# Float32r transposes of DMA-copied tiles in a one-core decoder block

## The chip, the core and the metric

The kernel runs on one core of one Trainium2 chip. A core has TensorE (PE, which multiplies matrices and transposes; its weight loads are listed apart as PEld), VectorE (DVE), ScalarE (ACT), GpSimd (POOL) and SyncE (SP), each with its own queue of instructions worked off in order. SP, ACT and POOL can start DMA transfers from their queues. The metric is the device time of one launch in microseconds (us), the median of three runs.

## The reference

One decoder layer on 256 rows of width 2048, all float32. An RMS norm and one wide input projection feed two branches: sparse attention (each query keeps 64 of its causal keys by an indexer score) and retention, whose output is normed by heads and gated. Both branches are projected up, weighted by sigmoid gates, added, projected by `w_out` and added to the input. A second RMS norm and an MLP with a squared ReLU follow:

```python
proj = rms_norm(x, ln1_g) @ w_in
o_attn = dsa_attention(...)
o_ret  = silu(rg) * group_norm_heads(retention_chunkwise(rq, rk, rv), ret_gn_g, ret_gn_b)
merged = sigmoid(ga) * (o_attn @ w_up_attn) + sigmoid(gb) * (o_ret @ w_up_ret)
x = x + merged @ w_out
h2 = rms_norm(x, ln2_g)
return x + square(relu(h2 @ w_ff1)) @ w_ff2
```

The change moves numbers about; what is computed stays.

## The kernel before, in words

**Products in three parts.** Every large product is made from float32r operands in three passes. `split` (line 343) turns a weight tile into a rounded part `whi` (ACT, line 359) and a rest `wlo` (DVE, line 360); activations are split likewise. `products` (line 401) then issues three matmuls for each 128 x 128 block of the activation: hi x hi (line 405), hi x lo (406), lo x hi (407), each with 512 moving columns. Weights stream in from memory over SP's queue, `LOAD_AHEAD` = 8 items ahead, and are split two or three items ahead. An item is a pair of k slices of a weight tile.

**Why there are transposes.** An activation is made with its rows on the partitions, but the next product needs its columns there. So a made tile of 128 x 512 is transposed by TensorE in four blocks of 128 x 128 against an identity matrix (`ident`, a float32 slice of `csb`) into a PSUM tile `pt`, from which `split_into` (line 424) makes the hi and lo parts, ACT at line 429 and DVE at line 430. `transpose_in` (line 432, the transposes at line 438) serves the retention output (called at line 955), the merged tiles (line 1010) and the MLP's activations (`hidden`, line 1123). `next_norm` (line 1035) transposes the rows of the second norm itself, at line 1048, with evictions at line 1050.

**Where they stand in the order.** The program walks the products item by item. Jobs beside them are generators in a list `work`; `step()` moves each by one `yield`, and it runs once for every k slice in `run_block` (six products) and once for every item in the merged stages (six products for a first-layer item, twelve for a second-layer item). A `transpose_in` waits some yields before it transposes: two by default, `W_GN` = 7 after the retention; `next_norm` waits one. From this program order and the dependences the build lays out each engine's queue. It may move an instruction past others of its queue, so in the trace a transpose can stand within a triple of products.

**The MLP.** The hidden width is worked in eight groups (g = 0 to 7). The first group is a plain product (line 1129). For each later group the program alternates first-layer items, in a scheme of seven half products instead of eight (`first`, line 792), with second-layer items of the group before (`second`, line 1161); `merged` (line 123) writes this order out. A group gives four tiles of 128 x 512: two after the fifth half product, one after the sixth and one after the seventh. Each gets ReLU and Square on ACT (`squared`, lines 1110 and 1111), is transposed, and is read by the second-layer items of the next stretch. These items' results are scaled by ACT (line 1184) and added to memory by an accumulating DMA from POOL (line 1185).

**Buffers.** Tiles of 128 x 512 come from `stage()` (line 200), which hands out eight buffers in turn: three of four calls take one of six in the pool `sp`, the fourth takes one of two in the pool in `late["stg"]`. A buffer is written again only when the readers of its last tile are done.

Of the kernel before, what the change touches and what calls it, by code (L numbers as in the profile page):

```python
# [10 lines left out]
F32 = mybir.dt.float32  # L11
F32R = mybir.dt.float32r
I32 = mybir.dt.int32
AF = mybir.ActivationFunctionType
# [3 lines left out]
P = 128  # L18
# [4 lines left out]
BN = 512  # L23
# [10 lines left out]
FG = 8  # L34
NG = DFF // (FG * P)
# [124 lines left out]
def block_kernel(ctx, tc, cst, rot, xt, gains, w, x, ret_gn_g, ret_gn_b, out):  # L160
    nc = tc.nc
# [3 lines left out]
    cp = ctx.enter_context(tc.tile_pool(name="cp", bufs=1))  # L165
# [23 lines left out]


    W_NORM, W_SOFT, W_GN = 3, 5, 7
    n_stg, n_mid, n_sm = 8, {"ep": 12, "e4": 20}, 24
    late = {"ep": ep, "stg": ep}
    n_stage = [0]

    def nm(s):
        uid[0] += 1
        return f"{s}_{uid[0]}"

    def stage(shape=(P, BN)):  # L200
        n_stage[0] += 1
        pool, bufs = (late["stg"], 2) if n_stage[0] % 4 == 0 and "stg" in late else (sp, n_stg - 2)
        return pool.tile(list(shape), F32, tag="stg", name=nm("stg"), bufs=bufs)

    def mid(shape, dtype=F32):
        return late["ep"].tile(list(shape), dtype, tag="mid", name=nm("mid"), bufs=n_mid[late["ep"].name])

    def small(w):
        return sp.tile([P, w], F32, tag="small", name=nm("small"), bufs=n_sm)

    def psum_t():
        return PS["pt"].tile([P, BN], F32, tag="pt", name=nm("pt"))
# [4 lines left out]
    def act_pair(slot):  # L217
        a = ap[slot].tile([P, DK, 2, S], F32R, tag="act", name=nm("act"))
        return a[:, :, 0, :], a[:, :, 1, :], a

    work = []
# [17 lines left out]
    xsb = [stage() for _ in range(T * 4)]  # L239
    csb = cp.tile([P, C_DEC], F32, name="csb")  # L240
    ident = csb[:, C_ID:C_ID + P]
    cmk = csb[:, C_CM:C_CM + P]


# [144 lines left out]
    def run_block(key, act, before=None, ps=None, k0=0, k1=None):  # L389
        nk, n = B[key]  # L390
        ps = ps or [PS["pm"].tile([P, BN], F32, tag="pm", name=nm("pm")) for _ in range(T)]
        for k in range(k0, k1 or nk):
            if k % HC == 0:
                ws = weights((key, k // KC, k % KC // HC))
            if before:
                before(k)
            step()
            products(ps, [p[:, :n] for p in (ws[0][:, k % HC], ws[1][:, k % HC])], [act(k, t) for t in range(T)], k == 0, k == nk - 1)
        return [p[:, :n] for p in ps]
# [9 lines left out]
    def of(a):  # L409
        return lambda k, t: tuple(z[:, k, t * P:(t + 1) * P] for z in a[:2])  # L410


    def rsqrt(v, n, mul):

        a, y, u = small(n), small(n), small(n)
        nc.vector.tensor_scalar(a, v, mul, EPS, op0=ALU.mult, op1=ALU.add)
        nc.vector.tensor_scalar(y.bitcast(I32), a.bitcast(I32), -0.5, float(0x5F3759DF), op0=ALU.mult, op1=ALU.add)
        for _ in range(3):
            nc.vector.tensor_tensor(u, y, y, op=ALU.mult)
            nc.vector.scalar_tensor_tensor(u, u, -0.5, a, op0=ALU.mult, op1=ALU.mult)  # L420
            nc.vector.scalar_tensor_tensor(y, u, 1.5, y, op0=ALU.add, op1=ALU.mult)
        return y

    def split_into(act, k0, nk, t, ps):

        src = ps.rearrange("p (c i) -> p c i", c=nk)
        hi = act[0][:, k0:k0 + nk, t * P:(t + 1) * P]
        lo = act[1][:, k0:k0 + nk, t * P:(t + 1) * P]
        nc.scalar.activation(hi, src, AF.Copy)
        nc.vector.tensor_tensor(lo, src, hi.bitcast(F32), op=ALU.subtract)  # L430

    def transpose_in(act, k0, t, src, wait=2):

        for _ in range(wait):
            yield
        ps = psum_t()
        for c in range(4):
            nc.tensor.transpose(ps[:, c * P:(c + 1) * P], src[:, c * P:(c + 1) * P], ident)  # L438
        split_into(act, k0, 4, t, ps)


# [32 lines left out]
    def evict(dst, ps, t, func=AF.Copy):  # L474
        nc.scalar.activation(dst, ps, func, scale=rows[t])

    def evicted(ps, t):
        a = stage()
        evict(a, ps, t)
        return a  # L480
# [34 lines left out]
    for i in range(3):  # L515
        ps = run_block(("I", i), of(hT)) if i else psI
        for t in range(T):
            evict(iqs[:, t, i * IN:(i + 1) * IN], ps[t], t)
    mb = []

    def indexer():
        ik2 = mid([P, T, 2, ID])
# [70 lines left out]
    ps = run_block(("AV", 0), of(hT))  # L593
# [67 lines left out]
    for j in range(NKV):  # L661
        ps = run_block(("AQ", j), of(hT))
# [82 lines left out]
    def scaled(b):  # L745

        assert late["X2 made"]
        late["scaled"] = b + 1
        z = late["X2"][:, b // 2, b % 2 * 4:b % 2 * 4 + 4]
        hi, lo = (hT[a][:, 4 * b:4 * b + 4, P:] for a in range(2))  # L750
        nc.scalar.activation(hi, z, AF.Copy)
        nc.vector.tensor_tensor(lo, z, hi.bitcast(F32), op=ALU.subtract)

    for which, key in ((0, "RQ"), (1, "RK")):
        for i in range(2):
            last = (which, i) == (1, 0)
            ps = run_block((key, i), of(hT), before=(lambda k: scaled(k // 4 - 1) if k in (4, 8, 12) else None) if last else None)
# [93 lines left out]
    for gate, u in ((z, u) for z in BESIDE for u in range(2)):  # L851
# [10 lines left out]
        for item in beside(gate, u):  # L862
# [7 lines left out]
            else:  # L870
                branch(item, of(oT if gate == "GA" else hT))
                i = item[0][1] - 2 * u
# [13 lines left out]
    rT = act_pair(1)  # L886
# [45 lines left out]
    def normed(j, ys, gb, sg):  # L932
        mv, vr, nb = small(4 * T), small(2 * T), small(2 * T)
        for t in range(T):
            for a in range(2):
                st = small(6)
                nc.vector.bn_stats(st, ys[t][:, a * RV:(a + 1) * RV])
                nc.vector.bn_aggr(mv[:, 4 * t + 2 * a:4 * t + 2 * a + 2], st)
        mean, var = (mv.rearrange("p (a b) -> p a b", b=2)[:, :, i] for i in range(2))
        nc.vector.tensor_copy(vr, var)  # L940
        yield
        r = rsqrt(vr, 2 * T, 1.0)
        nc.vector.scalar_tensor_tensor(nb, mean, -1.0, r, op0=ALU.mult, op1=ALU.mult)
        yield
        for t in range(T):
            y = ys[t]
            for a in range(2):
                c = slice(a * RV, (a + 1) * RV)
                i = 2 * t + a
                nc.scalar.activation(y[:, c], y[:, c], AF.Identity, scale=r[:, i:i + 1], bias=nb[:, i:i + 1])  # L950
            nc.vector.tensor_tensor(y, y, gb[0], op=ALU.mult)
            nc.vector.tensor_tensor(y, y, gb[1], op=ALU.add)
            yield
            nc.vector.tensor_tensor(y, y, sg[t], op=ALU.mult)
            work.append(transpose_in(rT, 4 * j, t, y, W_GN))

    for j in range(4):
        if j < 2:

            i = j  # L960
# [5 lines left out]
        for src in (ret_gn_g, ret_gn_b):  # L966
            g = mid([P, BN])
            nc.gpsimd.dma_start(g, src[:, j * BN:(j + 1) * BN].to_broadcast([P, BN]))
            gb.append(g)
        for t in range(T):  # L970
            z = mid([P, BN])
# [6 lines left out]
        ps = run_block(("RV", j), of(hT))  # L978
# [9 lines left out]
    mT = act_pair(0)  # L988
# [14 lines left out]
    for i in range(4):  # L1003
        ms = mss[i] if i in pair else gates(i)
        ps = run_block(("UR", i), of(rT), ps=pair.get(i), k0=len(PARTS[0]) * KC if i in pair else 0)
        for t, m in enumerate(ms):
            g = sgb[:, t, i * BN:(i + 1) * BN]
            nc.vector.tensor_tensor(g, ps[t], g, op=ALU.mult)
            nc.vector.tensor_tensor(m, m, g, op=ALU.add)
            work.append(transpose_in(mT, 4 * i, t, m))  # L1010


    x2 = px.tile([P, T, D], F32, tag="big2", name="x2")
# [21 lines left out]
    def next_norm(i):  # L1035

        xs = []
        for t in range(T):
            a = stage()
            nc.scalar.activation(a, x2[:, t, i * BN:(i + 1) * BN], AF.Copy, scale=rs[:, t:t + 1])  # L1040
            xs.append(a)
        yield
        half, c0 = divmod(4 * i, HK)
        for k in range(0, 4, 2):
            ps = psum_t()
            for c in range(2):
                for t in range(T):
                    nc.tensor.transpose(ps[:, (2 * c + t) * P:(2 * c + t + 1) * P], xs[t][:, (k + c) * P:(k + c + 1) * P], ident)
            for c in range(2):
                nc.scalar.activation(xr[half][:, :, c0 + k + c, :], ps[:, c * S:(c + 1) * S].rearrange("p (t s) -> p t s", t=T),  # L1050
                                     AF.Copy, scale=g2[:, 4 * i + k + c:4 * i + k + c + 1])
            yield
        for t in range(T):
            both(((X11, X21), (X12, X22))[half][t], xr[half][:, t:t + 1, c0:c0 + 4, :], 1, slice(c0, c0 + 4))
# [21 lines left out]
    for i in range(4):  # L1076
        ps = run_block(("O", i), of(mT))
        for t in range(T):
            z = x2[:, t, i * BN:(i + 1) * BN]
# [13 lines left out]
    hid = act_pair(0)  # L1093
# [26 lines left out]
    def form(f, k):  # L1120
        return tuple(xf[:, a, f, k, :] for a in range(2))

    def hidden(g, t, i):
        work.append(transpose_in([z[:, g % 2 * FG:] for z in hid[:2]], 4 * i, t, ys.pop((t, i))))

    blocks = ((X11, X21), (X12, X22))
    ys = {}
    for i in (1, 0):
        ps = run_block(("F1", i), lambda k, t: form(blocks[k // HK][t], k % HK))
# [107 lines left out]
```

## Time and profile before

| what | value |
|---|---|
| time, median of 3 runs | 1611.77 us (1611.72 to 1613.01) |
| span of the profiled execution, first to last instruction | 1609.7 us |
| time outside the span, against the median | 2.1 us |
| TensorE busy | 1603.1 us |
| TensorE's weight loads busy | 1334.0 us |
| VectorE busy | 1316.7 us |
| ScalarE busy | 1001.8 us |
| GpSimd busy | 90.9 us |
| moved by DMA | 351.80 MB |

The profiled execution is given by its span alone; what lies around it is taken as the 2.1 us by which the median is longer. A row of the page that groups instructions gives line, engine, operation, output <- inputs, shape and count, then busy time, mean length of one, and the engine's idle time just before with what ended it. A row of the chain of waits gives start, length, engine, output tile and line of a piece of the chain that ended last: the length there is what the piece adds to the end. A row of the timeline gives start, length as recorded, engine, line, operation and count; recorded lengths of matmuls overlap, since they are pipelined.

### The profile page before, as it was taken

The page shows a single profiled execution, that of the slowest core. Times are in us where ns is not written, and L with a number is a line of the kernel's source. Part 1 is how long each engine was busy: PE and PEld are TensorE (multiplying, and loading weights), DVE is VectorE, ACT ScalarE, POOL GpSimd, SP SyncE. Part 2 cuts the span into 40 slices and gives each one's busy share as a digit, 9 for nine tenths or more (in the row PEclk, how much of TensorE's full clock was granted, in tenths as well). Part 3 has the DMA queues.
Part 4 walks back from the last instruction along what each step waited for, and adds up shares of the span by engine and source line. Part 5 has one row for each costly group of instructions (what it writes and reads, how often), then busy time and mean ns, then how long its engine had stood idle before and what let it go on. Part 6 is the DMA issues. An engine that isn't in the chain of part 4 may idle for free.

```text
span 1609.7 us, 19743 instructions
## 1 busy us (share of the span) xinstructions
PE 1603.1 (100%) x7438; PEld 1334.0 (83%) x7438; DVE 1316.7 (82%) x1474; ACT 1001.8 (62%) x1236; POOL 90.9 (6%) x135
## 2 busy tenths in 40 slices
PE   9999999999999999999999999999999999999999
PEld 8978888888888888888888888888888888888887
DVE  6678889898989898688665589898989898989884
ACT  7556566566666666555444666766767676767672
POOL 0000000000000001202000000000000000000000
PEclk9999999999999999999999999999999999999999
DMA  9645346656565655857557574767676777777763
GB/s 331 221 148 183 131 144 248 220 216 230 202 257 207 264 200 181 320 202 261 184 203 255 204 274 145 248 197 254 207 250 198 241 227 235 235 235 234 218 201 133
DMA packets 68416, 351.80 MB, mean 219 GB/s; under 512 B 7776, under 2 KB 14560, under 8 KB 32736
## 3 DMA queue, kind: packets, MB, share of 16 engines
q1 hardware_dynamic: 51040, 308.96, 52.8%
q0 software_dynamic: 14256, 35.14, 10.0%
q10 hardware_dynamic: 3024, 6.44, 1.1%
q8 instruction: 58, 0.95, 0.2%
q14 instruction: 38, 0.31, 0.1%
HBM read 323.24 MB, written 27.26 MB: 218 GB/s over the span
## 4 chain that ended last, share of the span: by engine, by line
PE 96%; DVE 3%; DMA 0%; ACT 0%; issue 0%; ACTq 0%; DVEq 0%
PE pm L405 11%; PE pm L407 11%; PE pm L406 11%; PE pf L405 11%; PE pf L407 11%; PE pf L406 11%; PE pq L406 9%; PE pq L407 9%; PE pq L405 9%; PE pt L438 1%; DVE wlo L360 1%; PE pa L405 1%; PE pa L406 0%; PE pa L407 0%; PE pt L649 0%; PE pa L907 0%
## 5 line engine op out<-in xcount | busy, mean ns | idle before, releaser
L360 DVE TENSOR_TENSOR wlo<-raw,whi 128x1024 fp32r<-128x1024 f32 (+2 forms) x544 | 645.7, 1200 | 211.1 <-ACT whi L359 203.1
L359 ACT ACTIVATE whi<-raw 128x1024 fp32r<-128x1024 f32 (+2 forms) x544 | 563.3, 1042 | 406.5 <-PE pm L407 200.5
L405 PE MATMUL pm<-whi,act 128*128 128x512 f32 (+1 forms) x800 | 310.0, 388 | 0.3 <-ACT act L449 0.3
L406 PE MATMUL pm<-wlo,act 128*128 128x512 f32 (+1 forms) x800 | 306.5, 383 | 0.5 <-DVE wlo L360 0.5
L407 PE MATMUL pm<-whi,act 128*128 128x512 f32 (+1 forms) x800 | 307.0, 384 | 0.0
L405 PE MATMUL pf<-whi,act 128*128 128x512 f32 (+1 forms) x768 | 298.5, 390 | 0.0
L406 PE MATMUL pf<-wlo,act 128*128 128x512 f32 (+1 forms) x768 | 298.2, 388 | 0.0
L407 PE MATMUL pf<-whi,act 128*128 128x512 f32 (+1 forms) x768 | 298.1, 388 | 0.0
L360 DVE TENSOR_TENSOR wlo<-rawc,whi 128x1024 fp32r<-128x1024 f32 x176 | 214.7, 1220 | 43.6 <-ACT whi L359 41.4
L359 ACT ACTIVATE whi<-rawc 128x1024 fp32r<-128x1024 f32 x176 | 186.3, 1059 | 80.8 <-PE pf L407 35.8
L349 DVE TENSOR_TENSOR raw<-raw,raw 128x2048 f32<-128x2048 f32 x88 | 201.0, 2285 | 1.1 <-DMA raw<-in_w_dram 0.5
L407 PEld LDWEIGHTS pm<-whi,act 128*128 128x128 f32 x800 | 150.2, 188 | 27.8 <-DVE act L450 0.2
L405 PEld LDWEIGHTS pm<-whi,act 128*128 128x128 f32 x800 | 150.3, 188 | 26.9 <-ACT act L449 0.6
L406 PEld LDWEIGHTS pm<-wlo,act 128*128 128x128 f32 x800 | 150.3, 188 | 26.9 <-DVE wlo L360 1.1
L405 PEld LDWEIGHTS pf<-whi,act 128*128 128x128 f32 x768 | 144.1, 188 | 30.0 <-ACT whi L359 0.8
L407 PEld LDWEIGHTS pf<-whi,act 128*128 128x128 f32 x768 | 144.2, 188 | 29.8
L406 PEld LDWEIGHTS pf<-wlo,act 128*128 128x128 f32 x768 | 144.3, 188 | 29.5
L405 PE MATMUL pq<-whi,xf 128*128 128x512 f32 x392 | 154.4, 394 | 0.0
L407 PE MATMUL pq<-whi,xf 128*128 128x512 f32 x392 | 152.7, 390 | 0.0
L406 PE MATMUL pq<-wlo,xf 128*128 128x512 f32 x392 | 152.6, 389 | 0.0
L1185 POOL DMA_DIRECT2D sums<-ev x56 | 48.3, 943 | 777.2 <-ACT ev L1184 775.6
L407 PEld LDWEIGHTS pq<-whi,xf 128*128 128x128 f32 x392 | 73.6, 188 | 15.5
(206 smaller groups left out, 1520.3 us busy)
## 6 DMA issues: line engine op xcount, KB each, us to landing
raw<-in_w_dram SPq DMA_DIRECT2D x188, 1024.0 KB, 5.4
rawc<-in_w_dram SPq DMA_DIRECT2D x88, 1024.0 KB, 5.7
sums<-ev POOLq DMA_DIRECT2D x56, 256.0 KB, 5.5
raw<-in_w_dram SPq DMA_DIRECT2D x8, 736.0 KB, 4.8
raw<-in_w_dram SPq DMA_DIRECT2D x7, 512.0 KB, 7.0
raw<-in_w_dram SPq DMA_DIRECT2D x8, 368.0 KB, 7.4
stg<-in_x_dram SPq DMA_DIRECT2D x8, 256.0 KB, 7.6
rqkd<-stg POOLq DMA_DIRECT2D x8, 256.0 KB, 2.8
```

What stands on the lines that cost most here:

```text
L349: nc.vector.tensor_tensor(one, one, two, op=ALU.add)
L359: nc.scalar.activation(a, src, AF.Copy)
L360: nc.vector.tensor_tensor(b, src, a.bitcast(F32), op=ALU.subtract)
L405: nc.tensor.matmul(d, h, hi, start=first, stop=False, skip_group_check=skip)
L406: nc.tensor.matmul(d, h, lo, start=False, stop=False, skip_group_check=skip)
L407: nc.tensor.matmul(d, l, hi, start=False, stop=last, skip_group_check=skip)
L438: nc.tensor.transpose(ps[:, c * P:(c + 1) * P], src[:, c * P:(c + 1) * P], ident)
L1185: nc.gpsimd.dma_start(sums[:, t, i * BN:(i + 1) * BN], z, accum_op=ALU.add)
```

## The change

A float32r identity `unit` is made once, by an ACT copy of `ident`. A new helper `moved(src)` takes a stage tile of type float32r and starts a DMA on ACT's queue that copies `src` into it bit by bit. `turn` transposes a block: if the source is float32r, with `unit` and into the PSUM tile read as float32r; otherwise as before. Four callers use it:

- the retention's normed tiles, all copied; the wait goes from 7 yields to 10
- the merged tiles of blocks 0 to 2; their wait goes from 2 to `W_MOVED` = 6; those of block 3 stay as they were
- `next_norm`, all tiles; the wait goes from 1 to 6
- the MLP's tiles of all groups but the last; the wait goes from 2 to 6

```diff
+    W_MOVED = 6
...
-    def stage(shape=(P, BN)):
+    def stage(shape=(P, BN), dtype=F32):
         n_stage[0] += 1
         pool, bufs = (late["stg"], 2) if n_stage[0] % 4 == 0 and "stg" in late else (sp, n_stg - 2)
-        return pool.tile(list(shape), F32, tag="stg", name=nm("stg"), bufs=bufs)
+        return pool.tile(list(shape), dtype, tag="stg", name=nm("moved" if dtype == F32R else "stg"), bufs=bufs)
+
+    def moved(src):
+
+        z = stage(dtype=F32R)
+        nc.scalar.dma_start(z.bitcast(F32), src)
+        return z
...
+    unit = cp.tile([P, P], F32R, name="unit")
...
+    def turn(ps, c, src, i):
+
+        d, z = ps[:, c * P:(c + 1) * P], src[:, i * P:(i + 1) * P]
+        if src.dtype == F32R:
+            nc.tensor.transpose(d.bitcast(F32R), z, unit)
+        else:
+            nc.tensor.transpose(d, z, ident)
+
     def transpose_in(act, k0, t, src, wait=2):
...
         for c in range(4):
-            nc.tensor.transpose(ps[:, c * P:(c + 1) * P], src[:, c * P:(c + 1) * P], ident)
+            turn(ps, c, src, c)
         split_into(act, k0, 4, t, ps)
...
+    nc.scalar.activation(unit, ident, AF.Copy)
...
-            work.append(transpose_in(rT, 4 * j, t, y, W_GN))
+            work.append(transpose_in(rT, 4 * j, t, moved(y), W_GN + 3))
...
-            work.append(transpose_in(mT, 4 * i, t, m))
+            work.append(transpose_in(mT, 4 * i, t, *((moved(m), W_MOVED) if i < 3 else (m,))))
...
             nc.scalar.activation(a, x2[:, t, i * BN:(i + 1) * BN], AF.Copy, scale=rs[:, t:t + 1])
-            xs.append(a)
-        yield
+            xs.append(moved(a))
+        for _ in range(W_MOVED):
+            yield
...
-                    nc.tensor.transpose(ps[:, (2 * c + t) * P:(2 * c + t + 1) * P], xs[t][:, (k + c) * P:(k + c + 1) * P], ident)
+                    turn(ps, 2 * c + t, xs[t], k + c)
...
-        work.append(transpose_in([z[:, g % 2 * FG:] for z in hid[:2]], 4 * i, t, ys.pop((t, i))))
+        y = ys.pop((t, i))
+        work.append(transpose_in([z[:, g % 2 * FG:] for z in hid[:2]], 4 * i, t, *((moved(y), W_MOVED) if g < NG - 1 else (y,))))
```

## The prediction, on record before the result

> **What bounds the kernel now.** I read the page first, then busy time by stretches, then the chain of work in order of time around the transposes. The page:
>
> ```profile
> span 1609.7 us, 19743 instructions
> PE 1603.1 (100%) x7438; PEld 1334.0 (83%) x7438; DVE 1316.7 (82%) x1474; ACT 1001.8 (62%) x1236; POOL 90.9 (6%) x135
> ...
> DMA  9645346656565655857557574767676777777763
> ...
> PE 96%; DVE 3%; DMA 0%; ACT 0%; issue 0%; ACTq 0%; DVEq 0%
> PE pm L405 11%; PE pm L407 11%; PE pm L406 11%; PE pf L405 11%; PE pf L407 11%; PE pf L406 11%; PE pq L406 9%; PE pq L407 9%; PE pq L405 9%; PE pt L438 1%; DVE wlo L360 1%; PE pa L405 1%; PE pa L406 0%; PE pa L407 0%; PE pt L649 0%; PE pa L907 0%
> ```
>
> TensorE carries 96% of the chain, and the transposes of line 438 stand in it with 1%. A busy share alone does not say that nothing waits, so two stretches (length; PE, PEld, DVE, ACT, POOL busy; clock; DMA share; GB/s):
>
> ```profile
> 250.00:650.00 400.00, 399.96 (x1777) 330.19 (x1777) 360.47 (x322) 248.70 (x263) 23.79 (x42) 1.00 0.62 225
> 975.00:1609.00 634.00, 631.00 (x2860) 521.89 (x2858) 543.58 (x452) 429.30 (x488) 48.28 (x56) 1.00 0.68 216
> ```
>
> The clock is at 1.00 in both, and TensorE loses 0.04 us of 400 and 3 of 634. So what is taken off TensorE's stream shows in the time, one for one, as long as nothing new keeps it waiting. DVE, at 543.6 of 634 in the MLP, would be next, 87 us behind: far more than this change can move.
>
> **The price of a transpose.** The chain gives what one instruction costs the stream, not its latency (start, length, engine, tile, line):
>
> ```profile
> 689.95 0.23 PE pm L407
> ...
> 691.31 0.23 PE pm L407
> 691.54 0.44 PE pt L438 x4
> 691.98 0.23 PE pm L405
> ...
> 790.39 0.87 PE pt L438 x8
> ```
>
> Seven products of 512 columns lie between 689.95 and 691.54, 0.227 us each. Eight transposes of 128 columns take 0.87, 0.109 each, as do those at 691.54. All are float32; the products are float32r. A transpose in float32r is not in this trace, nor any float32r product of 128 columns. The nearest is 256 columns wide:
>
> ```profile
> L405 PE MATMUL pa<-mid,mid 128*128 128x256 f32 x24 | 6.8, 281 | 0.0
> ```
> ```profile
> 671.63 0.12 PE pa L405
> ...
> 672.34 0.24 PE pm L405
> ```
>
> Six of these fill 671.63 to 672.34, 0.118 each. So 256 columns are worth 0.227 - 0.118 = 0.109, and 128 fewer would make 0.118 - 0.054 = 0.064. That is the middle value. The bounds come from the weight loads, since each transpose needs one:
>
> ```profile
> 114.30 0.19 PEld L406 LDWEIGHTS pm<-wlo,act 128*128 128x128 f32 x1 [0.88 <-DVE wlo L360]
> 114.30 0.50 PE L406 MATMUL pm<-wlo,act 128*128 128x512 f32 x1 [0.46 <-DVE wlo L360]
> 114.41 0.19 PEld L407 LDWEIGHTS pm<-whi,act 128*128 128x128 f32 x1
> ```
> ```profile
> 912.91 0.14 PEld L1048 LDWEIGHTS pt<-csb,stg 128*128 128x128 f32 x1 [0.43 <-ACT stg L1040]
> 912.91 0.33 PE L1048 MATMUL pt<-csb,stg 128*128 128x128 f32 x1
> 912.91 0.24 PEld L407 LDWEIGHTS pm<-whi,act 128*128 128x128 f32 x1
> ```
>
> At 114.30 TensorE had been standing, and the next load came 0.11 later: a float32r product's load holds the loader 0.11. At 912.91, also after a stand, the load behind that of a transpose shows 0.24 where 0.19 is usual: a transpose's load holds it 0.05. If a float32r transpose keeps the short load, it can cost no less than about 0.055; if it loads like a product, 0.11, and no more than the 0.118 of the wide product. Plain float32 tells which is nearer:
>
> ```profile
> L630 PEld LDWEIGHTS pa<-kT,mid x32: 187/192/192, 145.0 to 231.2; 128*128 128x128 f32 x32
> L630 PE MATMUL pa<-kT,mid x32: 272/275/275, 145.3 to 231.3; 128*128 128x128 f32 x32
> ```
> ```profile
> 145.44 0.67 PE pa L630 x6
> ```
>
> Here a float32 product that is no transpose loads in 187 to 192 ns like every float32r product (0.19), not in 0.14. So the short load goes with the transpose and not with the type, and I take 0.064.
>
> How many: 8 normed tiles of the retention, 6 of the 8 merged tiles (i < 3), 8 of next_norm and 28 of the MLP's 32 (all groups but the last) are copied: 50 tiles, 4 transposes each, 200. At 0.109 - 0.064 = 0.045 they save 9.0 us; between 0.055 and 0.118 that is +10.8 to -1.8.
>
> The Trainium skill's page "TensorE: Matmul & The Clock Gate", section "Terms", speaks against this: its transpose mode makes FP32 four times faster, so a float32 transpose would already have all there is, the saving would be 0 and the time 1611.8. The trace has half of that: a plain float32 product of line 630 takes two records of 0.67 / 6 = 0.11, 0.22 together, and the transpose 0.109, twice as fast. The same page's section "Back-to-back issue gap" gives about 81 ns for a load with 128 moving columns in a stream; by it the saving would be 200 x 0.028 = 5.6 us and the time 1606.2, an estimate from that page that no row here shows.
>
> **The copies.** A SBUF-to-SBUF copy is not in the trace. Nearest are 256 KB writes:
>
> ```profile
> L1083 ACTq DMA_DIRECT2D sums<-x x8: 326/330/603, 862.4 to 931.4; - x8
> ...
> DMA to landing us min/median/max: 2.3/3.0/4.4
> ```
> ```profile
> L1185 POOL DMA_DIRECT2D sums<-ev x56: 844/862/1145, 1001.9 to 1562.7; - x56
> ...
> DMA to landing us min/median/max: 4.1/5.5/12.6
> ```
>
> The first goes out on ACT's queue as the copies will, the second is an accumulating write in the MLP's traffic. I take 3 to 4.4 us and keep 12.6 for the rival. The 50 copies move 13 MB at a DMA share of 0.68; I cost that at nothing, since weight loads run eight items ahead.
>
> Issuing costs ACT 50 x 0.33 = 16.5 us. A copy also waits on ACT's queue for its source, ACT's own Square in the MLP, DVE in the retention and the merge; behind it stand the casts of line 359, for which DVE's line 360 and then TensorE wait. The cover is ACT's idle time just before those casts (releaser: us, times):
>
> ```profile
>   PE pm L407: 203.9, 147
>   PE pf L407: 163.8, 110
>   PE pq L407: 59.3, 182
> ```
>
> ACT stands 427 us waiting for TensorE to free a weight buffer, about 1 us at each of 439 casts; a copy's issue and wait fit into one or two such gaps, and the cast is two items ahead. Without that cover it would be 16.5 us lost.
>
> **Are the tiles there in time?** A step is 6 products, 1.36 us, or 12, 2.72, for a second-layer item. Rows of producer and transpose:
>
> ```profile
> 1536.92 0.62 ACT L1111 ACTIVATE stg<-stg 128x512 f32<-128x512 f32 x1
> ...
> 1558.53 0.63 ACT L1111 ACTIVATE stg<-stg 128x512 f32<-128x512 f32 x1
> ```
> ```profile
> 1033.75 0.61 PE pt L438 x4
> ...
> 1537.76 0.49 PE pt L438 x4
> ...
> 1561.68 0.44 PE pt L438 x4
> ```
> ```profile
> 685.93 0.68 DVE L954 TENSOR_TENSOR stg<-stg,mid 128x512 f32<-128x512 f32 x1
> ```
> ```profile
> 693.37 0.44 PE pt L438 x4
> ```
> ```profile
> 788.41 1.28 DVE L1009 TENSOR_TENSOR mid<-mid,sgb 128x512 f32<-128x512 f32 x2
> ```
>
> MLP: waiting six steps for two moves the transposes by three first-layer items and one second-layer item, 6.8 us. Those at 1561.68 go to 1568.5, for a tile ready at 1559.2: 9.3 us. The pair at 1537.76 goes to 1544.6, for tiles ready at 1535.5 and 1537.5: 7 to 9 us. Retention: 6.8 us now (686.6 to 693.4) and 4.1 more. Merge: 0.7 us now (789.7 to 790.4) and 5.4 more. All exceed 0.33 + 4.4. The later end is also met: the last tile of a group is transposed one product item, one second-layer item and two product items (6.8 us) before its first reader.
>
> Two small terms remain. Seven of the MLP's bursts now stand for the Square, 0.17 us at 1033.75 (0.61 for 0.44) and 0.05 at 1537.76; that goes: at most 1.2 us. Against it next_norm: three of them start in one step and now ask for 12 stage tiles of 8, so the third's copies can only land after the first's transposes, 8 us into a block of 21.8, and need 3 to 4 us more. Where TensorE's queue holds those transposes too early it stands, for 1 us perhaps. The two cancel. Sum: 1609.7 - 9.0 = 1600.7 for the span; the median shown, 1611.8, lies 2.1 above the span, and with the same around it the time is 1602.8.
>
> **The rivals.** First, float32r buys a transpose nothing: it loads like a product (0.11) or passes at the pace of float32. For it: the 0.11 at 114.30. Against: the short load stays with the transpose, and the 256-column row shows float32r at half the float32 price per column. Time: 1611.8, between 1610 and 1613.6. The rule of the Trainium skill's section "Terms" leads there too. Second, load and pass of a float32r transpose overlap only in part, since in so short an instruction the load of 0.05 is as long as the pass, and it lands midway between 0.064 and 0.109, at 0.087: 200 x 0.022 = 4.4 us, 1607.4. For it: the wide products cost more than their columns (0.118 for columns worth 0.109). Against: today's transposes stand at 0.109 without a trace of it. Third, on the other side, late copies: if a copy in the MLP takes over 9 us, as the worst of the accumulating writes did, TensorE stands at each of three bursts in seven groups. A mean of 0.43 us at 21 bursts eats the 9.0; at 1 us each it is 21 - 9 = 12 us slower, 1623.8. Against: the median of those writes is 5.5, and ACT's own writes never passed 4.4.
>
> **How the numbers follow.** A measurement of this kernel tells 0.2%, 3.2 us, from no change. The forecast of 9.0 has 0.67, the half gain 0.05, no gain 0.17, late copies or a dearer transpose 0.11. So faster 0.72, same 0.17, slower 0.11. The forecast's own range is 1601 (0.055 each) to 1605. The whole reaches over no gain, to 1612, and leaves out the late copies and a few in a hundred below.
>
> **What would show it.** In the chain after, four float32r transposes at about 0.26 instead of 0.44, the last group's at 0.44 still; PE's sum of busy time 9 us less; copies landing in 3 to 5 us; ACT issuing 50 times 0.33; no new waits of TensorE on a DMA. If the four stay at 0.44, the first rival holds; if they shrink and the time does not, look for TensorE waiting on copies in the MLP or in next_norm.

## The result and the profile after

| | before | changed |
|---|---|---|
| time, median of 4 runs each | 1611.74 us (1611.44 to 1613.01) | 1622.33 us (1621.51 to 1627.46) |
| span of the profiled execution | 1609.7 us | 1620.4 us |

The ratio is 1.0072, with a 95% interval of 1.006 to 1.0084: 10.6 us slower. The forecast was 1602.8 us with a range up to 1612. One execution of f1 below (3268.64 us) and two of g2 (4027.79 and 7807.18 us) took far longer than the rest, and the medians given leave them out. In the changed kernel the three products are lines 413 to 415, the splits 367 (ACT) and 368 (DVE), the copy 209, the float32r transposes 444, the scaling of the normed rows 1057.

The page after, with the chain by engine last:

```profile
PE 1602.4 (99%) x7438; PEld 1332.3 (82%) x7438; DVE 1314.7 (81%) x1474; ACT 1003.5 (62%) x1237; POOL 90.7 (6%) x135
...
PE 94%; DVE 3%; DMA 2%; ACT 1%; issue 0%; ACTq 0%; DVEq 0%
```

DMA has come into the chain: 2% where it had 0%. TensorE's busy time fell by only 0.7 us (1603.1 to 1602.4) while the span grew by 10.7. TensorE's waits (engine, tile, line, what it waited for: us, times, longest) name the place:

```profile
PE pt L444 <- DMA moved<-stg: 9.3, 4, 4.0
PE pt L517 <- DVE stg L511: 1.1, 4, 0.6
...
PE pf L414 <- DVE wlo L368: 1.0, 1, 1.0
PE pm L413 <- ACT act L465: 1.0, 1, 1.0
PE pm L414 <- DVE wlo L368: 0.8, 2, 0.5
```

Before, the same list held, beside a wait on line 246 that is unchanged:

```profile
PE pt L501 <- DVE stg L495: 0.9, 3, 0.6
PE pm L406 <- DVE wlo L360: 0.5, 1, 0.5
PE pm L405 <- ACT act L449: 0.3, 1, 0.3
```

Four waits for copies, 9.3 us, are new; the others grew by 2.2 in all (1.0 + 0.7 + 0.3 + 0.2). By stretches, in the columns that the prediction explained:

```profile
914.00:920.00 6.00, 2.04 (x11) 1.35 (x10) 0.00 (x0) 1.31 (x3) 0.00 (x0) 0.98 0.92 283
920.00:926.00 6.00, 6.00 (x25) 4.86 (x25) 1.23 (x1) 3.44 (x7) 0.00 (x0) 0.74 0.17 63
946.00:951.00 5.00, 1.48 (x8) 1.00 (x7) 2.41 (x3) 1.03 (x1) 0.00 (x0) 0.94 1.01 403
905.00:975.00 70.00, 60.38 (x268) 47.99 (x267) 42.63 (x67) 43.55 (x68) 0.00 (x0) 0.95 0.63 228
1015.00:1600.00 585.00, 585.00 (x2642) 483.70 (x2641) 508.28 (x422) 406.86 (x462) 48.11 (x56) 1.00 0.74 238
```

From 1015 to 1600 us, nearly the whole MLP, TensorE loses nothing. In the 70 us from 905 to 975, where the second norm's rows and the first MLP group are made, it loses 9.6, and behind the first long stand its granted clock is 0.74 on average. Cut into single microseconds, that clock is 0.50 from 920 to 923 us (and from 951 to 953, behind the second long stand), and 1.00 soon after:

```profile
921.00:922.00 1.00, 1.00 (x4) 0.71 (x4) 0.00 (x0) 1.00 (x2) 0.00 (x0) 0.50 0.45 168
...
924.00:925.00 1.00, 1.00 (x8) 0.81 (x7) 0.00 (x0) 0.35 (x1) 0.00 (x0) 1.00 0.00 0
```

The chain in order of time shows the first long stand:

```profile
912.39 7.30 DMA moved<-stg
...
919.73 0.62 PE pt L444 x3
920.36 0.55 PE pm L414
920.91 0.43 PE pm L415
...
923.05 0.32 PE pm L414
```

A copy of 7.3 us; three transposes at once behind it; then seven products (the five from 920.91 on at 0.43 each) in 3.0 us where 1.6 is usual. The transposes are slow as well. The second long stand, 3.5 us at 950.59, is followed by the same. The two tails together are some 2.7 us, once the 0.07 that a transpose always leaves on the product behind it is taken off in each.

In undisturbed stretches a burst of transposes now reads:

```profile
1064.27 0.29 PE pt L444 x4
1064.56 0.30 PE pf L413
1064.86 0.23 PE pf L414
```

Four read 0.29, and the product behind them 0.30 where 0.23 is usual. So the 0.29 is not the whole price: from 1064.27 to 1064.86 are 0.59 for four transposes and one product of 0.227, which leaves 0.363, or 0.091 each. Before, four took 0.44 with no such mark on the product behind (691.54 to 691.98), 0.110 each. The saving is 0.019 each.

**The balance.** Against the span before: +9.3 for the stands on copies, +2.7 for the slow products, +2.2 for other waits, -3.8 for 200 transposes at 0.019 less. That makes 10.4; measured were 10.7. The slow transposes of the two tails, and the waits for Square that went, are not in the sum.

### The profile page after: what moved, and what is told of

Its sections match the earlier page's. It is cut to its first block, busy times and chain, and to the rows that moved or that the text cites. A ratio compares the mean times of both kernels' runs of the same rounds, so it can differ in the third digit from the quotient of the medians.

```text
span 1620.4 us, 19835 instructions
## 1 busy us (share of the span) xinstructions
PE 1602.4 (99%) x7438; PEld 1332.3 (82%) x7438; DVE 1314.7 (81%) x1474; ACT 1003.5 (62%) x1237; POOL 90.7 (6%) x135
## 4 chain that ended last, share of the span: by engine, by line
PE 94%; DVE 3%; DMA 2%; ACT 1%; issue 0%; ACTq 0%; DVEq 0%
PE pf L413 11%; PE pf L414 11%; PE pf L415 11%; PE pm L413 10%; PE pm L415 10%; PE pm L414 10%; PE pq L413 9%; PE pq L414 9%; PE pq L415 9%; DMA moved<-stg 1%; DVE wlo L368 1%; PE pt L444 1%; PE pa L413 1%; PE pa L414 0%; PE pa L415 0%
## 5 line engine op out<-in xcount | busy, mean ns | idle before, releaser
L414 PEld LDWEIGHTS pf<-wlo,act 128*128 128x128 f32 x768 | 144.3, 188 | 30.9 <-DVE wlo L368 1.5
```

The lines of the kernel that those rows point to most:

```text
L414: nc.tensor.matmul(d, h, lo, start=False, stop=False, skip_group_check=skip)
```

## The experiments

My theory after the result: the copies of the second norm, perhaps those of MLP group 0 too, land after TensorE's queue asks for them, and a float32r transpose saves 0.019 us and not 0.045. The rivals: the rest of the change costs time too, or the float32r type itself does. The times of the kernel before are those taken beside each run.

**One part alone, and all but that part.** In e1 the second norm is put back:

```diff
-            xs.append(moved(a))
-        for _ in range(W_MOVED):
-            yield
+            xs.append(a)
+        yield
```

> next_norm is as before (no copies, one yield); retention, merge and MLP copied as in the change. Theory A (the loss is TensorE standing for copies in the stretch of next_norm and the first MLP tiles; a float32r transpose in a burst of four costs 0.0915 us against 0.1105, 0.019 less): 42 tiles x 4 x 0.019 = 3.2 us gained, 1608.5 us; up to 1610.6 if the 1.0 and 1.1 us stands at the first MLP tiles stay. Rival B (every copy costs, through ACT's queue and DMA traffic: 10.6 + 3.8 = 14.4 us over 50 copies): 42/50 of it stays, 1620.6 us.

Measured: 1616.15 us beside 1611.71, ratio 1.0026 (1.0016 to 1.0037). Neither number came. e2 does the opposite: only the second norm is copied.

```diff
-            work.append(transpose_in(rT, 4 * j, t, moved(y), W_GN + 3))
+            work.append(transpose_in(rT, 4 * j, t, y, W_GN))
...
-            work.append(transpose_in(mT, 4 * i, t, *((moved(m), W_MOVED) if i < 3 else (m,))))
+            work.append(transpose_in(mT, 4 * i, t, m))
...
-        work.append(transpose_in([z[:, g % 2 * FG:] for z in hid[:2]], 4 * i, t, *((moved(y), W_MOVED) if g < NG - 1 else (y,))))
+        work.append(transpose_in([z[:, g % 2 * FG:] for z in hid[:2]], 4 * i, t, y))
```

> The kernel before with next_norm's copies, float32r transposes and six yields alone. Theory A: 10 to 12.7 us of stands less 32 x 0.019 = 0.6, so 1621 to 1624 us, with the stands at the first transposes and at the last next_norm as after the whole change. Rival B: 8/50 of 14.4 us less 0.6, 1613.4 us.

Measured: 1619.37 beside 1611.71, ratio 1.0046 (1.0032 to 1.006). The second norm alone costs 7.7 us, less than the theory's 9 to 12: its two stands were 2.2 us each, where the change has 4.0 and 3.5. But in e1 the waits of TensorE did not go, they moved:

```profile
PE pt L444 <- DMA moved<-stg: 4.2, 2, 2.6
PE pf L414 <- DVE wlo L368: 1.3, 1, 1.3
```

The chain of e1 shows where:

```profile
956.18 8.36 DMA moved<-stg
964.67 0.72 PE pt L444 x4
965.39 0.55 PE pm L413
```

These are copies of MLP group 0. In the changed kernel they had made TensorE wait for only 0.9 and 1.0 us (at 972.15 and 975.05), behind the stands of the norm; without those, group 0's stands grew to 4.2 us in two pieces, with slow products behind them. So there were two places, and the first covered part of the second.

**The transposes without copies.** In e3 the operation that makes a tile (ACT's scaling or Square, DVE's product or sum) writes a float32r tile, which rounds it. There is no copy, and the waits are those of the kernel before; the transposes stay float32r. One of the four places:

```diff
-            nc.vector.tensor_tensor(y, y, sg[t], op=ALU.mult)
-            work.append(transpose_in(rT, 4 * j, t, moved(y), W_GN + 3))
+            z = stage(dtype=F32R)
+            nc.vector.tensor_tensor(z, y, sg[t], op=ALU.mult)
+            work.append(transpose_in(rT, 4 * j, t, z, W_GN))
```

> No copies: the tiles are written as float32r by ACT or DVE where they are made (so they are rounded to float32r there, which the reference does not do), and transposed as float32r with the waits of before. It measures the transpose alone. Theory A: 200 x 0.019 = 3.8 us gained, 1607.9 us. The price that the prediction took (0.064 each): 9.0 us, 1602.7 us. Rival (no gain in float32r): 1611.7 us.

Measured: 1609.70 beside 1611.71, ratio 0.9987 (0.9978 to 0.9995): 2.0 us faster. My price of 0.064 would have given 9. The theory's 3.8 is not all there either: its waits on other engines are 0.8 us longer in all than those of before (on `wlo` 1.0 for 0.5, on line 511 1.2 for 0.9), and the remaining 1 us I can't place.

**The copies without the type.** In e4 everything is copied and waits as in the change, but the tiles are float32 and so are the transposes:

```diff
-        z = stage(dtype=F32R)
-        nc.scalar.dma_start(z.bitcast(F32), src)
+        z = stage()
+        nc.scalar.dma_start(z, src)
```

> All 50 copies and all longer waits of the change, but into float32 tiles that are transposed in float32 as before. It measures the copies alone. Theory A: the changed kernel plus 3.8 us, 1626 us, with the same stands at next_norm. Rival C (the float32r transposes themselves bring the loss): under 1614 us.

Measured: 1622.81 beside 1611.71, ratio 1.0076 (1.0059 to 1.0093), as slow as the change. Its first wait:

```profile
PE pt L446 <- DMA stg<-stg: 6.6, 4, 3.7
```

The loss is with the copies, whatever the type. It did not come to the 1626 of the sum because the stands were 2.7 us shorter here than in the change.

**Both late places put back.** f1 is e1 and, besides, MLP group 0 uncopied; the retention, the merge and MLP groups 1 to 6 stay copied, 38 tiles with 152 transposes:

```diff
-... *((moved(y), W_MOVED) if g < NG - 1 else (y,))))
+... *((moved(y), W_MOVED) if 0 < g < NG - 1 else (y,))))
```

> next_norm and the four tiles of the MLP's group 0 as before; retention, merge and groups 1 to 6 copied: 152 float32r transposes. Theory D (all of the loss is stands behind copies made while the DMA engines are full, from the last output block to the end of the plain first-layer blocks): no stand there, 152 x 0.019 = 2.9 us gained, 1608.8 us; up to 1610.4 if the 1.6 us stand at the first merged items belongs to something else. Rival B (copies cost everywhere): over 1613 us.

Measured: 1608.82 beside 1611.76, ratio 0.9981 (0.9972 to 0.999). The same kernel was run again as g1, beside g2, which is f1 with float32 tiles and transposes (the edit of e4). The profile of this kernel shown below is g1's.

> The same kernel as f1_group0_uncopied (next_norm and group 0 as before, 38 tiles copied), once more for its profile and a narrower interval. Theory D: 1608.8 us again; in the profile no stand of TensorE on a copy, four float32r transposes at 0.37 us of the stream, copies landing in up to 8 us without a wait, and the 1.6 us stand on wlo at the first merged items gone, since nothing of group 0 is copied ahead of the casts on ACT's queue.

> The kernel of f1_group0_uncopied with its 38 copies and longer waits kept, but into float32 tiles that are transposed in float32. It prices the copies where they are in time. Theory D (in time they cost nothing): the kernel before, 1611.7 us, within 0.5. Rival B (each copy costs through ACT's queue and the DMA engines, and the float32r transposes win more than 0.019 each): clearly above 1612.5 us.

Measured: g1 1608.88 and g2 1611.68 beside 1611.64, ratios 0.9983 (0.9974 to 0.9992) and 1.0001 (0.9991 to 1.001). g2 says that 38 copies that land in time cost nothing, to within 1.6 us. g1 beside g2 gives the price of the type alone: 2.8 us over 152 transposes, 0.018 each. Two of the waits of g1, which has no stand on `wlo` for a `pf`:

```profile
PE pm L414 <- DVE wlo L368: 0.6, 2, 0.5
PE pt L444 <- DMA moved<-stg: 0.4, 1, 0.4
```

and a burst in the chain of g1, then of g2:

```profile
1373.80 0.30 PE pt L444 x4
1374.10 0.30 PE pq L413
```
```profile
1375.21 0.44 PE pt L446 x4
```

**Longer waits instead of no copies.** f4 puts the second norm back and gives group 0 a wait of ten steps; f2 gives ten steps to both, with the third and fourth block of the norm uncopied, so that buffers are less short:

```diff
-            xs.append(moved(a))
-        for _ in range(W_MOVED):
+            xs.append(moved(a) if i < 2 else a)
+        for _ in range(10 if i < 2 else 1):
             yield
...
-... *((moved(y), W_MOVED) if g < NG - 1 else (y,))))
+... *((moved(y), W_MOVED if g else 10) if g < NG - 1 else (y,))))
```

> next_norm as before; group 0 of the MLP copied, with ten steps of wait in place of six; the rest as in the change. Against the kernel with next_norm uncopied (1616.2 us) this undoes only the early use of two tiles. Theory D, too early: the stands of 1.7 and 2.9 us and 1.7 us of slow clock go, 168 x 0.019 = 3.2 us gained on the kernel before: 1608.5 us, up to 1610.1 with the 1.6 us at the first merged items. If these copies are late for another reason (they wait behind something on ACT's queue), the stands move along and it stays at 1614 to 1616 us.

> Copies where the DMA engines are full, but with ten steps in place of six: next_norm 0 and 1 (2 and 3 are as before, so that buffers are less short) and group 0 of the MLP; the rest as in the change. Theory D with 'asked for too early' as the cause: ten steps, 13.6 us, exceed the 6 to 10 us that these copies take, so the stands go; 184 x 0.019 = 3.5 us gained, 1608.2 us, to 1610 with rests. If the buffers are the cause, next_norm keeps a stand of about 4 us and 1.4 us of slow clock: 1613 us or more.

Measured: f4 1609.34 beside 1611.76, ratio 0.9984 (0.9975 to 0.9993); f2 1610.90 beside 1611.76, ratio 0.9996 (0.9987 to 1.0005). In both the waits for copies are gone, so lateness was the cause and more steps cure it. What is left in f4 is one stand in its timeline (in square brackets the idle time before, and what ended it):

```profile
982.66 0.50 PE L414 MATMUL pf<-wlo,act 128*128 128x512 f32 x1 [1.31 <-DVE wlo L368]
```

It is in the change and in e1 too (1.0 and 1.3 us), and not in g1: it goes with the copies of group 0, at the first second-layer items. In f2 something else stands, in its timeline:

```profile
920.10 0.72 ACT L1057 ACTIVATE stg<-x,rs 128x512 f32<-128x512 f32 x1 [3.27 <-DMA moved<-stg]
...
920.88 0.87 PE L446 MATMUL pt<-csb,stg 128*128 128x128 f32 x6 [1.93 <-ACT stg L1057]
```

The rows of an uncopied block want a stage buffer that a copy is still reading: ACT waits 3.27 us for it, and TensorE 1.9 for ACT. In the change ACT stood for a buffer in the same way, 3.86 us until 919.71. The eight buffers are the second price of a copy, since it holds two at once.

**The slow products.** f3 puts sixteen plain float32 products of 128 columns, which feed nothing, ahead of the transposes of the norm's first and last block, so that TensorE would have work in the stands:

```diff
+        if i % 3 == 0:
+            fill = psum_a()
+            for _ in range(16):
+                nc.tensor.matmul(fill[:, :P], warm, warm, start=True, stop=True)
```

> The changed kernel with 16 plain float32 products of constants (0.22 us each, 3.5 us, of no use to the output) ahead of the transposes of next_norm 0 and 3, where TensorE stands 4.2 and 3.8 us. If standing still costs the clock afterwards (products at 0.43 instead of 0.23 us after each stand), the fillers take the place of the stand and the clock stays: 2.6 us faster than the change, about 1619.7 us. If the slow products have another cause, no gain: 1622.3 us or later.

Measured: 1630.68 beside 1611.76, ratio 1.0113 (1.0099 to 1.0126). The products did not stay in the stands: the build let them run earlier, and the waits are as in the change:

```profile
PE pt L444 <- DMA moved<-stg: 9.4, 6, 3.8
```

They cost the stream 64 records of 0.11, 7.0 us of the 8.4, and the products behind the stands are still slow. So it doesn't show whether work in the stands would keep the clock up.

## Why the prediction was wrong

The method held: TensorE bounds the kernel, what is taken off its stream shows one for one (f1: 152 x 0.019 = 2.9 expected, 2.9 and 2.8 measured), and what stands in front of it shows as well. Two steps failed, and the second made the sign wrong.

**The term of 200 x 0.045 = 9.0 us was mis-sized.** It measured 200 x 0.019 = 3.8 us (0.018 by g1 and g2). I took the short load of 0.05 for a property of the transpose, as plain float32 products load in 0.19. The timeline of the changed kernel shows the loader:

```profile
1386.76 0.40 PEld L444 LDWEIGHTS pt<-unit,moved 128*128 128x128 f32 x4 [0.23 <-issue]
...
1387.10 0.19 PEld L413 LDWEIGHTS pq<-whi,xf 128*128 128x128 f32 x1
```

Four loads hold it for 0.34, from 1386.76 to the next load at 1387.10: 0.085 each, neither the 0.05 nor the 0.11 of my two bounds. That the load sets this pace, and not the pass, is a reading that fits and that no run tests alone. What speaks for it is a lone float32r transpose, in the chain of the change where the clock is full again:

```profile
926.53 0.06 PE pt L444
926.59 0.28 PE pm L415
```

It is over in 0.06, the pass of 64 ns that I derived from the columns, but the product behind it takes 0.28 for 0.23. That makes 0.11, as much as a product's load held the loader at 114.30, and no less than a float32 transpose costs. Three loads of 0.085 and one of 0.11 make 0.365 for a burst of four, where 0.363 was read. The second rival (0.087, "load and pass overlap only in part") had this size, and I gave it 0.05. The Trainium skill's page "TensorE: Matmul & The Clock Gate", section "Back-to-back issue gap", with its 81 ns for a load and 128 columns in a stream, was also nearer than my 64: the trace has 85 ns by the loader and 91 by the stream. I had it in hand and weighed it at nothing, because no row showed it; but no row showed my 64 ns either. The same page's section "Terms", by which float32 transposes would have nothing left to gain, is not borne out.

**"Are the tiles there in time?" was answered from the wrong place.** I worked the margins out for the MLP's steady groups, the retention and the merge, and they held: no wait there. The copies' rows after, from issue to landing, first from 905 to 975 us, then from 1030 to 1600:

```profile
L209 ACTq DMA_DIRECT2D moved<-stg x10: 472/472/755, 911.8 to 968.6; - x10
...
DMA to landing us min/median/max: 2.2/6.5/10.3
...
L209 ACTq DMA_DIRECT2D moved<-stg x24: 472/472/473, 1044.6 to 1486.2; - x24
...
DMA to landing us min/median/max: 2.3/5.2/8.2
```

The 3 to 4.4 us lay between the best and the middle of both groups, not at the worst. In the steady groups the copies took up to 8.2 and were covered by 7 to 9. For the other two places:

- *next_norm, "for 1 us perhaps".* It measured 7.5 us of stands (4.0 + 3.5) and their slow tails. The row I quoted at 912.91 already held the warning: the weight load of the norm's first transpose stood 0.43 for the very ACT that scales the rows. TensorE itself lost nothing by it, but there was no margin to begin with, and six steps are counted from the program, not from when ACT is done. In the changed kernel's timeline the first copy goes out at 911.78 and TensorE's queue has come to the transposes at 914.58:

```profile
911.78 1.14 ACTq L209 DMA_DIRECT2D moved<-stg  x2
...
914.58 0.14 PEld L444 LDWEIGHTS pt<-unit,moved 128*128 128x128 f32 x1
...
919.73 0.62 PE L444 MATMUL pt<-unit,moved 128*128 128x128 f32 x3 [3.96 <-DMA moved<-stg]
```

That leaves 2.8 us. The first tile of the pair was there, the second only 7.3 us after it had set out, and in the stretch from 914 to 920 the DMA share is 0.92. I had seen the shortage of buffers (12 for 8) and its place, but not that the copies would take 7 to 9 us there.

- *Group 0.* I gave it the margin of the others. But it is a plain product, whose step is six products, 1.36 us, with no second-layer item among them: six steps are 8.2 us, from which ReLU, Square and the issue come off before the copy sets out. The timeline of e1 shows what was left:

```profile
953.52 0.48 ACTq L209 DMA_DIRECT2D moved<-stg  x1
...
961.52 0.51 PE L444 MATMUL pt<-unit,moved 128*128 128x128 f32 x4 [1.55 <-DMA moved<-stg]
```

TensorE's queue had come to the transposes at 961.52 - 1.55 = 959.97, 6.4 us after the issue, and the copies needed about 8 (961.52 - 953.52). At ten steps they were in time (f4).

**"I cost that at nothing": the DMA share.** The mean of 0.68 was taken over the 634 us from 975 on, and the long stands came before that, in stretches of 0.92 and 1.01. There a copy shares the DMA engines with the weight loads: from 914 to 920 us the packets of the weights' queue took 60.9% of their time and those of the copies' queue 30.9%. These are the same stretches in which a copy is needed soonest.

**"The two cancel": the small terms.** They did not: the removed waits for Square were 1.2 at most, the norm and group 0 cost 12.

**The price of ACT's queue.** An issue took 0.47 and not 0.33, 23.6 us for 50. The cover held; ACT's idle time just before its casts, by what ended it, in the changed kernel:

```profile
  PE pm L415: 202.5, 142
  PE pf L415: 168.9, 116
  PE pq L415: 57.1, 178
```

These are 428.5 us where it was 427.0. Only at one place did it fail, the 1.0 to 1.3 us on `wlo` that go with group 0's copies.

**The third rival**, late copies, was right in kind and got most of its place wrong: I put it at 21 bursts in seven groups of the MLP, and priced it from a copy "over 9 us". It came at two bursts of the second norm, which are not among the 21, and at two of group 0's, for copies of 6 to 10 us; in the other six groups the covers held. A chance of 0.11 for it and a dearer transpose together was far too little for the mechanism that made the sign.

The half pace behind a stand is that of the granted clock, 0.50 in the slices from 920 to 923 and 951 to 953 us of the change and from 963 to 969 of e1. Not settled is which stands bring it. The rows show it behind stands of 4.0 and 3.5 us, in e2 behind two of 2.2, in e1 behind 1.6 and 2.7 close together, and not behind the 1.9 of f2 or the 0.9 and 1.0 in the change. f3 did not test what brings it, as its products ran ahead of the stands.

## What to carry to other kernels

A step that is put between a producer and its reader has to be checked at each place where the reader stands closest behind, not at the typical one: a burst that already waits for its producer in the trace has no margin, and a copy there is paid in full. Take a transfer's time from the DMA share of the stretch in which it runs, and count the buffers that it holds. And when the work taken off is priced from wider or other instructions, put the load beside the pass, since the slower of the two may set the price. Here the version that keeps only the covered copies (f1, 1608.82 us) gains 2.9 us, 0.18%, all that float32r has to give there, with an interval that just excludes no change.

## What the runs showed of the hardware

- A float32r transpose of 128 x 128 holds the weight loader 0.085 us and costs TensorE's stream 0.091 in a burst of four; 0.07 of the burst shows only in the product behind it.
- A copy of 256 KB within SBUF, issued by ACT, landed in 2.2 us at best and in 10.3 at worst in the same 70 us, in which the DMA share swung from 0.17 to 1.01. In f4's stretch from 955 to 965 us the share was 0.99 and a copy took up to 7.8 us, yet TensorE was busy throughout, because nobody asked for the tiles sooner:

```profile
955.00:965.00 10.00, 10.00 (x46) 8.29 (x45) 4.52 (x4) 5.77 (x7) 0.00 (x0) 1.00 0.99 393
```

- After a stand TensorE can run at half pace: 0.43 for a product of 512 columns instead of 0.23, for about 3 us, with a granted clock of 0.50 there. The Trainium skill's page "TensorE: Matmul & The Clock Gate", section "What's actually happening", has the clock halve after an idle window of about 3.4 us. The two long stands of the change agree with it; in e2 a stand of 2.19 us was enough, as the chain of e2 shows:

```profile
947.24 0.34 PE pt L444 x2
...
948.73 0.55 PE pm L414
949.28 0.43 PE pm L415
```

So a wait of 2.2 us can cost 1.4 more behind it, and the length that decides is not settled by these runs.
